# Attention as steps of three parts in a written order on TensorE, in one layer step of a hybrid trunk

## The chip, the cores and the metric

The kernel runs on one core of a Trainium2 chip. The metric is the device time of one execution in microseconds (us): 3321.58 us median of three runs of the kernel before (3320.39 to 3327.34). Engines are named as in the profile: PE is TensorE (matmuls), PEld its weight loads, DVE is VectorE, ACT is ScalarE, POOL is GpSimd, SP issues the DMAs.

## The reference, cut to what matters

Two layers work on 512 latent and 128 prompt tokens of width 1024. Each layer has a feed-forward half step, a mixer and another feed-forward half step; the change is in the mixer. It adds three kinds of heads to the residual stream through one output projection:

```python
x = x + g1 * (0.5 * swiglu(modulate(rms_norm(x, ...), sh1, sc1), ffn1_w1, ffn1_w2))
m, aux = mix_fn(modulate(rms_norm(x, lp['norm_mix']), sh2, sc2))   # [MLA | SWA | GatedDeltaNet] @ w_out
x = x + g2 * m
x = x + g3 * (0.5 * swiglu(modulate(rms_norm(x, ...), sh3, sc3), ffn2_w1, ffn2_w2))

# MLA, 8 heads: every latent token sees all 512 latent tokens and 128 cached ones; prompt sees prompt
s = (einsum(q_nope, k_nope) + einsum(q_rope, k_rope)) * scale
o = einsum(softmax(s), v)
# SWA, 8 heads on 2 key heads: latent tokens see a band of three 128 blocks, the cache and a sink
s = where(valid, einsum(q, k) * scale, -inf);  p = softmax([s_loc, s_ctx, sink])
# gated delta net (GDN), 4 heads, forward and backward: a scan over chunks of 64 tokens
tinv = triangular_solve(eye + lower, eye);  u = tinv @ (v * beta);  wk = tinv @ (kb * exp(gc))
v_new = u_i - w_i @ s;  o_i = qd_i @ s + a_i @ v_new;  s = s * gt_i + kd_i.T @ v_new
```

## The kernel before

All tensors lie with features on the 128 partitions and the 640 tokens (512 latent, 128 prompt) along the free side. The program is written in a framework that places instructions by a simulated schedule: each engine gets one fixed order of instructions, chosen at build time, and waits on semaphores. Tiles come from pools with a number of buffers; a new tile waits until the last reader of the buffer before it is done.

A mixer projects its inputs (`win`, line L104), and does the GDN heads one after the other as groups 0 to 3; a fifth group, group 4, holds the prompt's tokens of all four heads. A group (`gdn_group`, from line 597) has a preparation (norms L615, transposes L634 and L638, decay and products L645 to L672, a 16-step substitution on DVE L692 to L694, its spreading by ACT L710, and products by TensorE L703 with DVE L715 and L720 between them), a recurrence (`step`, L742 to L746) and a tail (L776 to L796). The products of a preparation use two PSUM banks of the kind G; the recurrence uses one bank each of the kinds S0 and S1. PSUM has eight banks: here L=4, G=2, S0=1, S1=1.

After the last projections (`project`, from line 806) the banks of kind L are given up and attention takes their place, with two banks for scores (S) and two for transposes and values (T) in SWA, and, once G, S0 and S1 are given up, with two double banks for scores and four of kind T in MLA.

A head of attention does this: TensorE writes scores of 128 queries into an S tile (L981, L985 mask, L1006 prompt; MLA L1036); DVE takes the row maximum (L905) and its negative (L907 or L909); ACT takes the exponentials (L910) and their sum; DVE takes the reciprocal (L914, with the sink L912, L913); POOL multiplies (L915) into a tile `pr`. Then `pv` transposes `pr` block by block on TensorE into T tiles (L931), ACT copies these to SBUF (L938), TensorE multiplies by the values into another T tile (L942), and ACT copies that to the output (L944). Two blocks of queries share one `pv`; a head has two such pairs, and the prompt's block is a third, smaller one. In the trace a matmul of f32 operands shows as two passes, one of fp32r operands as one.

The order of attention on TensorE is the scheduler's: calls stand in the code as scores, softmax and `pv` of one pair after the other, and the schedule moves them between each other and between the GDN's instructions, as far as tiles allow. Group 4's recurrence and preparation are in the code ahead of attention and are mixed with it.

Outputs of heads go to DRAM (`do`). Before MLA head 2 the buffers of the GDN are given up, a pool for the 24 halves of the outputs is opened in their place, and nine outputs are loaded back (`of<-do`, L507) and split into a high and a low part (ACT L67, DVE L70). MLA heads 2 to 7 are split directly. Then the output projection begins (L104 again, with six L banks).

## Time and profile before

| | |
|---|---|
| median of 3 runs | 3321.58 us |
| the profiled execution's own time | 3325.07 us |
| its span in the trace | 3323.3 us |
| PE busy | 3241.5 us, 98% of the span |
| DVE, ACT, POOL busy | 1886.3, 1384.8, 452.2 us |
| mean granted TensorE clock | 0.987 of 2.4 GHz |
| granted clock and DMA | between 1000 and 1100 us: 0.95 and a DMA share of 0.46 |

A busy PE is not a PE at its peak: ends of matmuls are modelled and overlap, so a stretch that shows hardly any idle time may hold less work than it could. The time is best read stage by stage, by the instructions that begin and end a stage. The stage that is changed begins, in layer 0, near 892 us (group 4's preparation) and ends where the output projection begins, at 1113 us; in layer 1 the same stage runs from 2529 to 2749 us.

### The profile page before, as it was taken

The numbers are of one execution on the slowest core, as the hardware profiler recorded it, in microseconds if no ns is written. First come the engines' busy times: TensorE is split into PE (matmuls) and PEld (weight loads), VectorE is DVE, ScalarE is ACT, GpSimd is POOL, SyncE is SP. The second block draws the span as 40 slices with busy tenths as digits, with TensorE's granted clock in tenths as the row PEclk, the third lists the DMA queues.
The fourth block names the chain that finished last, engine by engine and source line by source line (L and its number), as shares of the span: only waits on it lengthen the run. The fifth ranks groups of instructions, "written<-read, shape, count | busy, mean of one in ns | idle before, by whom it ended". The sixth has DMA issues, their size and how long they took to land.

```text
span 3323.3 us, 56733 instructions
## 1 busy us (share of the span) xinstructions
PE 3241.5 (98%) x22036; PEld 3129.5 (94%) x22036; DVE 1886.3 (57%) x4357; ACT 1384.8 (42%) x3041; POOL 452.2 (14%) x480
## 2 busy tenths in 40 slices
PE   8999999999998999999999999999999989999998
PEld 5999999999887999999999999999998879999998
DVE  4564577686885355643346735477878653433333
ACT  3332334554676433322233323255466763321222
POOL 0000011222343100100000100012114340000000
PEclk9999999999999999999999999999999999999999
DMA  6443453322714224522224534333235242222222
GB/s 212 128 149 116 134 164 127 97 76 91 201 54 138 84 86 133 155 94 72 69 92 143 156 99 139 98 103 110 72 121 152 75 138 74 69 73 74 83 65 76
DMA packets 180190, 364.78 MB, mean 110 GB/s; under 512 B 28112, under 2 KB 68176, under 8 KB 179920
## 3 DMA queue, kind: packets, MB, share of 16 engines
q1 hardware_dynamic: 179920, 361.15, 35.2%
q8 instruction: 173, 2.83, 0.4%
q14 instruction: 97, 0.79, 0.1%
HBM read 315.03 MB, written 46.04 MB: 109 GB/s over the span
## 4 chain that ended last, share of the span: by engine, by line
PE 87%; DVE 6%; ACT 3%; DMA 2%; issue 2%; SPq 0%; POOL 0%; POOLq 0%; DVEq 0%; ACTq 0%
PE psL L104 72%; PE psT L942 3%; PE psG L703 3%; PE psS L1036 2%; PE psT L931 1%; PE psG L275 1%; PE psS L742 1%; DMA of<-do 1%; PE psS L745 1%; ACT pr L910 1%; PE psS L981 1%; DVE hf L169 1%; DMA adaw<-in_wada_dram 0%; DVE wlo L70 0%; PE psS L776 0%
## 5 line engine op out<-in xcount | busy, mean ns | idle before, releaser
L70 DVE TENSOR_TENSOR wlo<-wr,whi 128x512 fp32r<-128x512 f32 (+2 forms) x726 | 494.2, 682 | 709.5 <-ACT whi L67 708.0
L67 ACT ACTIVATE whi<-wr 128x512 fp32r<-128x512 f32 (+2 forms) x726 | 446.2, 616 | 876.2 <-PE psL L104 614.9
L104 PE MATMUL psL<-hb,whi 128*128 128x320 f32 x1968 | 523.8, 313 | 0.7 <-DVE hb L171 0.5
L104 PE MATMUL psL<-hc,whi 128*128 128x320 f32 x1952 | 521.0, 314 | 0.0
L104 PE MATMUL psL<-ha,whi 128*128 128x320 f32 x1856 | 492.3, 312 | 5.0 <-DVE ha L171 3.7
L104 PE MATMUL psL<-hd,whi 128*128 128x320 f32 (+1 forms) x1856 | 486.3, 310 | 1.9 <-DVE hd L171 1.9
L104 PE MATMUL psL<-mh,wlo 128*128 128x320 f32 x1408 | 434.2, 309 | 0.0
L104 PE MATMUL psL<-ml,whi 128*128 128x320 f32 x1408 | 434.0, 309 | 0.0
L104 PE MATMUL psL<-mh,whi 128*128 128x320 f32 x1408 | 432.9, 310 | 0.0
L104 PEld LDWEIGHTS psL<-hb,whi 128*128 128x128 f32 x1968 | 351.9, 189 | 2.6 <-DVE hb L171 1.2
L104 PEld LDWEIGHTS psL<-hc,whi 128*128 128x128 f32 x1952 | 349.4, 189 | 0.8
L104 PEld LDWEIGHTS psL<-ha,whi 128*128 128x128 f32 x1856 | 329.8, 188 | 8.6 <-DVE ha L171 5.7
L104 PEld LDWEIGHTS psL<-hd,whi 128*128 128x128 f32 (+1 forms) x1856 | 328.9, 188 | 5.2 <-DVE hd L171 3.1
L269 DVE SCALAR_TENSOR_TENSOR ada<-adaw,cs,ada 128x512 f32<-128x512 f32 x448 | 313.7, 743 | 0.0
L104 PE MATMUL psL<-hb,wlo 128*128 128x320 f32 (+1 forms) x984 | 307.3, 312 | 0.0
L104 PE MATMUL psL<-hc,wlo 128*128 128x320 f32 (+1 forms) x976 | 305.6, 313 | 0.0
L104 PE MATMUL psL<-hd,wlo 128*128 128x320 f32 (+1 forms) x928 | 287.7, 310 | 0.0
L104 PE MATMUL psL<-ha,wlo 128*128 128x320 f32 (+1 forms) x928 | 287.5, 311 | 0.0
L104 PEld LDWEIGHTS psL<-ml,whi 128*128 128x128 f32 x1408 | 264.0, 188 | 2.8
L104 PEld LDWEIGHTS psL<-mh,whi 128*128 128x128 f32 x1408 | 263.5, 188 | 3.0
L104 PEld LDWEIGHTS psL<-mh,wlo 128*128 128x128 f32 x1408 | 264.1, 188 | 2.0
L273 POOL TENSOR_TENSOR adal<-ada,adah 128x512 fp32r<-128x512 f32 x64 | 89.8, 1404 | 1041.7 <-ACT adah L67 823.3
(299 smaller groups left out, 5612.1 us busy)
## 6 DMA issues: line engine op xcount, KB each, us to landing
adaw<-in_wada_dram SPq DMA_DIRECT2D x288, 256.0 KB, 2.9
wr<-in_w1a_dram SPq DMA_DIRECT2D x88, 512.0 KB, 3.7
wr<-in_w1b_dram SPq DMA_DIRECT2D x88, 512.0 KB, 3.5
wr<-in_win_dram SPq DMA_DIRECT2D x54, 512.0 KB, 3.5
wr<-in_w2a_dram SPq DMA_DIRECT2D x32, 512.0 KB, 4.0
wr<-in_w2b_dram SPq DMA_DIRECT2D x32, 512.0 KB, 3.5
wr<-in_wo_dram SPq DMA_DIRECT2D x16, 512.0 KB, 3.6
dqn<-hd SPq DMA_DIRECT2D x24, 320.0 KB, 3.1
```

Source lines behind the costliest of these rows:

```text
L67: self.nc.scalar.activation(dst, src, AF.Copy)
L70: self.nc.vector.tensor_tensor(dst, src, hi.bitcast(F32), ALU.subtract)
L104: i = nc.tensor.matmul(p[:m, :cw], lhsT=w[:, :m], rhs=r[:, c0:c0 + cw], start=(k == 0 and n == 0), stop=(k == kt - 1 and n == 2))
L169: nc.vector.scalar_tensor_tensor(t[:, c0:c0 + n], self.x[k][:, s], A[:, k, g:g + 1], r[j][:, c0:c0 + n], ALU.mult, ALU.mult)
L269: nc.vector.scalar_tensor_tensor(acc[g], raw, c, acc[g], ALU.mult, ALU.add)
L273: nc.gpsimd.tensor_tensor(lo, acc[g], hi.bitcast(F32), ALU.subtract)
L275: nc.tensor.matmul(ps[:2, :], lhsT=self.sel[:, g, :], rhs=x, start=(g + n == 0), stop=(g + n == 2))
L703: nc.tensor.matmul(p[:, s], lhsT=lhs[:, s], rhs=rhs[:, s], start=True, stop=True)
L742: nc.tensor.matmul(p1[:, :P], lhsT=qw[:, u, c, 64 * d:64 * d + P], rhs=S, start=True, stop=True)
L745: nc.tensor.matmul(p2[:, :P], lhsT=KD_[d][c][:, us], rhs=UU[d][:, us], start=True, stop=True)
L942: nc.tensor.matmul(po[:, oc:oc + w], lhsT=vv[:, vb, :], rhs=hl[ti][:, s0:s0 + w], start=(n == 0), stop=(n == len(place) - 1))
L1036: nc.tensor.matmul(p[:, j, :w], lhsT=x[:96, qc], rhs=y[:96, k0 + j * w:k0 + j * w + w], start=(i == 0), stop=(i == 2))
```

## The change

Attention is now a list of steps. A step is a generator of three parts: the scores and softmax of one pair (or of a prompt block), the transposes with ACT's copies, and the values. `staged` runs through the list and, for step i, issues the scores of step i, then the transposes of step i-3, then the values of step i-4, all in a block in which TensorE's instructions keep the order in which they are written (`manual_schedule(engines={PE})`); the other engines are scheduled as before. GDN's last tail (`norm`, `output`), the widening of the score banks from one to two each (`widen`) and the loading of the nine outputs (`collect`) are steps of the same list. A head's order becomes first pair, prompt, second pair.

The PSUM banks change with it. L and G are both given up ahead of attention, while S0 and S1 stay until `widen`. Attention has four T banks and two S banks from its start: the four T banks are those of L, and the two S banks those of G. In MLA the score tiles take the two S banks and those of S0 and S1. Softmax has more buffers (`sm` 12 for 8; `pr` 6 for the wide tiles and 3 of its own for the prompt's, for 5 in all).

```diff
-        self.enter_banks(G=2, S0=1, S1=1, side="right")
+        scan = self.banks(S0=1, S1=1, side="right")
+        scan.__enter__()
+        self.enter_banks(G=2, side="right")
         self.enter_banks(L=4)
...
         self.leave_banks()
+        self.leave_banks()
         self.hp_close()
...
-        with self.banks(S=2, T=2):
-            self.swa(l)
-            t = tail("S0", "T")
-            next(t)
-        self.leave_banks()
-        self.enter_banks(S=2, T=4)
-        self.mla(l, range(2), hook=lambda: list(t))
+        def widen():
+            last.pop().__exit__(None, None, None)
+            scan.__exit__(None, None, None)
+            last.append(self.banks(S=2))
+            last[0].__enter__()
+            yield
+            yield
...
+        def collect():
+            self.leave()
+            self.wp = self.enter("wo")
+            for i in (8, 9, 10, 11, 4, 5, 6, 7):
+                fetch(i)
+            yield
+            yield
+            fetch(0)
+
+        steps = [*self.swa(l), norm(), widen(), *self.mla(l, 0), output(), *self.mla(l, 1), collect()]
+        for head in range(2, 8):
+            steps += self.mla(l, head, osplit)
+        with self.banks(T=4):
+            last.append(self.banks(S=2))
+            last[0].__enter__()
+            self.staged(steps)
+            last.pop().__exit__(None, None, None)
...
-        sm = lambda n: self.att.tile([P, 2], F32, tag=n, name=self.nm(n), bufs=8)
-        pr = self.att.tile([P, w], F32, tag="pr", name=self.nm("pr"), bufs=5)
+        sm = lambda n: self.att.tile([P, 2], F32, tag=n, name=self.nm(n), bufs=12)
+        pr = self.att.tile([P, w], F32, tag="pr" if w > P else "pp", name=self.nm("pr"), bufs=6 if w > P else 3)
...
             hl.append(f)
+        yield
         po = self.pt("T")
...
+    def staged(self, steps):
+        with self.tc.manual_schedule(engines={PE}):
+            n = len(steps)
+            for i in range(n + 4):
+                for at in (i, i - 3, i - 4):
+                    if 0 <= at < n:
+                        next(steps[at], None)
...
+        def latent(pair):
+            if pair == 0:
+                load()
+            vv, ot = self.pair
+            prs = [fin(n, 0, 2, 320) for n in (2 * pair, 2 * pair + 1)]
+            yield
+            blocks = [(s, [(prs[j], s * P, j) for j in range(2)]) for s in range(5)]
+            yield from self.pv(blocks, vv, ot, r0, pair * 256, 256)
...
+        return [latent(0), prompt(), latent(1)]
```

Two places show what moves. The first is TensorE's order where group 4's preparation begins in layer 0. Before, the first scores of SWA (L981, tiles `psS` from keys `k` and queries `q`) stand between the transposes of group 4's keys (L634) and of its values (L638); `uu` and `kd` belong to group 3's recurrence:

```order
L615 MATMUL psG_9517<-ones,QK_9524 128x2 x4
L634 MATMUL psG_9543<-mats,k_9509 128x128 x4
L745 MATMUL psS_1645_9058<-uu_9035,kd_8841 128x128
L981 MATMUL psS_10521<-k_10508,q_10518 128x256
L981 MATMUL psS_10521<-k_10509,q_10518 128x256
...
L981 MATMUL psS_10538<-k_10508,q_10518 128x384
...
L638 MATMUL psG_9544<-mats,v_9510 128x128 x4
L742 MATMUL psS_1647_9070<-st_9054,wqb_8471 128x128
L645 MATMUL psG_9557<-k_9509 128x128 x4
```

Now, on the same engine, the preparation's instructions follow each other with the recurrence alone between them (L645, L664, L668 and L675 are the old L615, L634, L638 and L645; L772 and L775 the recurrence), and the first scores (L1030) stand behind the preparation's last product (L733, the old L703):

```order
L645 MATMUL psG_9520<-ones,QK_9527 128x2 x4
L664 MATMUL psG_9546<-mats,k_9512 128x128 x4
L775 MATMUL psS_1646_9061<-uu_9038,kd_8844 128x128
L668 MATMUL psG_9547<-mats,v_9513 128x128 x4
L772 MATMUL psS_1648_9073<-st_9057,wqb_8474 128x128
...
L733 MATMUL psG_9794<-vn_9558,TT_9769 128x128 x4
L775 MATMUL psS_1804_9819<-uu_9784,kd_9590 128x128
L772 MATMUL psS_1805_9825<-st_9807,wqb_9511 128x128
L1030 MATMUL psS_10530<-k_10517,q_10527 128x256
```

All of SWA has moved behind the whole of group 4's preparation; 64 rows of TensorE's order that hold no attention stand there now.

The second place is a pair of MLA, again on TensorE. Before, the last scores of a pair (L1036) are followed by values (L942) and transposes (L931) in turn:

```order
L1036 MATMUL psS_12738<-k_12713,q_12716 128x320
L942 MATMUL psT_12625<-pt_12619,vv_12571 128x256 x2
L931 MATMUL psT_12664<-mats,pr_12639 128x128
L931 MATMUL psT_12664<-mats,pr_12655 128x128
...
L942 MATMUL psT_12625<-pt_12621,vv_12571 128x256 x2
L931 MATMUL psT_12669<-mats,pr_12639 128x128
...
L942 MATMUL psT_12625<-pt_12623,vv_12571 128x256
```

Now all scores of a pair stand together, then all transposes (L961) of the pair three steps back, then the values (L973) of the step four back, here a prompt's, and then the scores of the next head (L1102):

```order
L1102 MATMUL psS_12611<-k_12501,q_12504 128x320
L961 MATMUL psT_12627<-mats,pr_12451 128x128
L961 MATMUL psT_12627<-mats,pr_12467 128x128
...
L961 MATMUL psT_12632<-mats,pr_12451 128x128
...
L961 MATMUL psT_12637<-mats,pr_12451 128x128
...
L973 MATMUL psT_12646<-pt_12586,vv_12207 128x128
L1102 MATMUL psS_12661<-k_12652,q_12649 128x320
```

Scores of two pairs, four tiles, have one set of transposes and one short value product between them at this place.

## Rows read from the trace of the kernel before

**Rows 1.** The page, part 1: busy time, share of the span, instructions.

```profile
PE 3241.5 (98%) x22036; PEld 3129.5 (94%) x22036; DVE 1886.3 (57%) x4357; ACT 1384.8 (42%) x3041; POOL 452.2 (14%) x480
```

**Rows 2.** Timeline and chain, stage borders: start us, us, engine line op.

```profile
892.01 1.88 PE L615 MATMUL psG<-ones,QK 128*128 128x2 f32 x16
1113.24 11.87 PE psL L104 x81
2528.87 1.84 PE L615 MATMUL psG<-ones,QK 128*128 128x2 f32 x16
2749.45 30.65 PE psL L104 x209
```

**Rows 3.** Windows: us, busy PE, PEld, DVE, ACT, POOL, PEclk, DMA.

```profile
892.00:969.00 77.00, 70.31 (x494) 62.40 (x493) 63.50 (x245) 51.98 (x164) 34.90 (x39) 0.96 0.36 88
969.00:1004.00 35.00, 34.48 (x239) 30.45 (x239) 23.92 (x87) 28.22 (x87) 13.66 (x16) 1.00 0.21 64
1004.00:1064.00 60.00, 47.88 (x274) 42.23 (x272) 32.27 (x75) 36.09 (x84) 21.03 (x20) 0.91 0.47 134
1064.00:1104.00 40.00, 39.65 (x259) 36.81 (x258) 21.00 (x59) 30.17 (x74) 19.95 (x19) 1.00 0.44 133
2638.00:2700.00 62.00, 51.14 (x290) 44.49 (x289) 32.82 (x78) 38.47 (x90) 22.45 (x21) 0.92 0.49 137
```

**Rows 4.** Groups of instructions, DVE, 892 to 969 us: SWA's four.

```profile
L905 DVE TENSOR_REDUCE mx<-psS 128x1 f32<-128x384 f32 (+2 forms) x27 | 14.9, 553 | 3.7 <-PE psS L985 3.3 <-PE psS L1006 0.2
L913 DVE TENSOR_TENSOR den<-den 128x1 f32<-128x1 f32 x25 | 6.3, 252 | 2.2 <-ACT den L912 1.8
L907 DVE TENSOR_SCALAR nb<-mx,nsink 128x1 f32<-128x1 f32 x27 | 5.5, 204 | 0.3
L914 DVE RECIPROCAL den<-den 128x1 f32<-128x1 f32 x25 | 3.9, 154 | 0.1
```

**Rows 5.** Timeline, preparations of groups 2 (781), 3 (869) and 4 (915).

```profile
781.13 0.31 DVE L683 STREAM_TRANSPOSE u<-w 128x128 f32<-128x128 f32 x1 [0.88 <-ACT w L682]
796.71 0.48 DVE L697 TENSOR_SCALAR X<-X,half 128x128 f32<-128x128 f32 x2
869.61 0.48 DVE L697 TENSOR_SCALAR X<-X,half 128x128 f32<-128x128 f32 x2
890.89 1.06 PE L703 MATMUL psG<-vn,TT 128*128 128x128 f32 x8
915.00 0.29 DVE L683 STREAM_TRANSPOSE u<-w 128x128 f32<-128x128 f32 x1
940.08 0.47 DVE L697 TENSOR_SCALAR X<-X,half 128x128 f32<-128x128 f32 x2
968.72 0.50 PE L703 MATMUL psG<-vn,TT 128*128 128x128 f32 x3
```

**Rows 6.** Timeline and groups, SWA's prompt scores, and recurrence passes between them.

```profile
974.72 0.42 PE L1006 MATMUL psS<-k,q 128*128 128x128 f32 x2
994.32 0.52 PE L1006 MATMUL psS<-k,q 128*128 128x128 f32 x2
L742 PE MATMUL psS<-st,wqb 128*128 128x128 f32 x18 | 3.7, 289 | 0.0
```

**Rows 7.** Chain that ended last, dense MLA: start us, us, passes.

```profile
1078.42 0.87 PE psT L931 x8
1079.29 0.88 PE psS L1036 x6
1080.17 0.87 PE psT L942 x4
```

**Rows 8.** Waits of ACT, 1004 to 1064 us: us in total, times, longest.

```profile
ACT oh L67 <- DMA of<-do: 7.6, 4, 2.5
```

**Rows 9.** Timeline, from the end of one MLA score tile.

```profile
1080.21 0.82 DVE L905 TENSOR_REDUCE mx<-psS 128x1 f32<-128x640 f32 x1 [1.11 <-PE psS L1036]
1081.42 0.88 ACT L910 ACTIVATE pr<-psS,nb,rq 128x640 f32<-128x640 f32 x1
```

More of the change, by code (lines that the diff above doesn't have):

```diff
@@ new lines, in mixer, with norm, output, osplit @@
+        o = {}
+        first, last = tail("S0", "T"), []
+        def norm():
+            next(first)
+            yield
+            yield
+        def output():
+            yield
+            list(first)
+            yield
[6 more added lines that the diff above has]
+            yield
+        def osplit(i, f):
+            hi, lo = (self.wp.tile([P, T], F32R, tag="o", name=self.nm("o"), bufs=24) for _ in range(2))
+            self.split(f, hi, lo)
+            o[i] = (hi, lo)
@@ new lines, in mixer @@
+        for head in range(2, 8):
[5 more added lines that the diff above has]
+            last.pop().__exit__(None, None, None)
+        acm.__exit__(None, None, None)
+        self.hp_open()
+        self.open_x()
+        for k in range(KD):
+            nc.sync.dma_start(self.x[k], self.xd[k])
+        with self.banks(L=6, G=2):
+            order = (8, 9, 10, 11, 4, 5, 6, 7, 0, 1, 2, 3)
+            for n in range(KD):
+                w = self.weight(a['wo'][l, n, :, 8:], 4, P) + self.weight(a['wo'][l, n, :, :8], 8, P)
+                w = w[:4] + w[8:] + w[4:8]
+                self.residual(n, w, [o[i] for i in order], G, True)
@@ L939, in pv @@
             hl.append(f)
+        yield
         po = self.pt("T")
@@ L1011, in mla, with queries @@
-    def mla(self, l, heads, wp=None, osplit=None, hook=None):
-        nc, a, att = self.nc, self.a, self.att
-        for head in heads:
-            r0 = 64 * (head % 2)
-            rows = slice(r0, r0 + 64)
-            q, k = [], []
+            K[kv] = kh, kl, vv
+        def queries(head):
+            r0 = 64 * (head % 2)
+            if head % 2 == 0:
+                Q[head // 2, 'out'] = att.tile([P, T], F32, tag="out", name=self.nm("out"), bufs=2)
+            qh = att.tile([P, T], F32R, tag="q", name=self.nm("q"), bufs=4)
+            for n in range(2):
+                self.move(qh[64 * n:64 * n + 64], self.dsq[head // 2][n][r0:r0 + 64])
+            Q[head] = qh
@@ new lines, in latent @@
+        def latent(head, pair):
+            if pair == 0:
+                if head % 4 == 0:
+                    keys(head // 4)
+                queries(head)
+            kh, kl, vv = K[head // 4]
+            info = []
+            for n in (2 * pair, 2 * pair + 1):
+                p, w, lo, nl = scores(Q[head], kh, kl, n)
+                info.append((fin(head, p, w), lo, nl))
+            yield
+            blocks = [(4, [(info[j][0], info[j][2] * P, j) for j in range(2)])]
+            single = []
+            for b in range(4):
+                parts = [(info[j][0], (b - info[j][1]) * P, j) for j in range(2)
+                         if info[j][1] <= b < info[j][1] + info[j][2]]
+                if len(parts) == 2:
+                    blocks.append((b, parts))
+                elif parts:
+                    single.append((b, parts))
+            ot = Q[head // 2, 'out']
+            yield from self.pv(blocks + single, vv, ot, 64 * (head % 2), pair * 256, 256)
+            if pair == 1 and head % 2 == 1:
+                nc.sync.dma_start(self.do[4 + head // 2], ot)
@@ new lines, in prompt @@
+        def prompt(head):
+            kh, kl, vv = K[head // 4]
+            p = self.pt("S")
+            for n, x in enumerate((kh, kl)):
+                nc.tensor.matmul(p[:, :P], lhsT=Q[head][:, TL:], rhs=x[:, T:], start=(n == 0), stop=(n == 1))
+            pr = fin(head, p, P)
+            yield
+            ot = Q[head // 2, 'out']
+            yield from self.pv([(5, [(pr, 0, 0)])], vv, ot, 64 * (head % 2), TL, P)
+        return [s for head in range(8) for s in (latent(head, 0), prompt(head), latent(head, 1))]
@@ L1017, in mla, with load @@
+    def mla(self, l, head, osplit=None):
+        nc, att = self.nc, self.att
+        r0 = 64 * (head % 2)
+        rows = slice(r0, r0 + 64)
+        q, k = [], []
+        def load():
             for n in range(2):
```

140 lines of the change are left out of this document (48 added, 92 removed).

## The prediction

> **What bounds the kernel now.** I read the page's busy shares first [rows 1]: TensorE shows 98%, DVE 57%, ACT 42%, so a change pays where TensorE's order leaves it short of work. Then the chain of waits and the timeline, for the stage's borders: from the first norm of group 4's preparation to the output projection it is 1113.24 - 892.01 = 221.2 us in layer 0 and 2749.45 - 2528.87 = 220.6 us in layer 1 [rows 2]. Then the windows [rows 3], which show three kinds of stretch. From 892 to 969 us SWA runs beside group 3's recurrence and group 4's preparation: TensorE is busy 70.3 of 77 us, but DVE 63.5, and that is the engine that sets this pace. From 969 to 1004 and from 1064 to 1104 us TensorE is busy 34.5 of 35 and 39.7 of 40 us: nothing is left to win there. From 1004 to 1064 us, where MLA starts and the nine outputs are loaded back, it idles 12.1 of 60 us, at a granted clock of 0.91; in layer 1 (2638 to 2700) 10.9 of 62 us, at 0.92.
>
> So the new order can win only in the first and third kind of stretch. In the third it does what it is good for, distance between scores, transposes and values. In the first it takes SWA out: the S banks are now those of G, so the first score stands behind the last product of group 4's preparation, and TensorE gets group 3's recurrence and that preparation alone. One overlap is given up, another gained.
>
> **The change part by part, for one layer.**
>
> *The preparation alone.* Before, 892.01 to 969.2 us, 77 us. DVE spent 14.9 + 6.3 + 5.5 + 3.9 = 30.6 us of it on SWA's softmax [rows 4]. If all of that and nothing else went, 77 - 30.6 = 46.4 us would be left: the lower bound. For the middle I cut it into legs [rows 5]. Norm to DVE's transpose of the triangles (915.00): 23.0 us; with SWA's reductions out of DVE's queue, about 18. The 16-step substitution, 915.00 to 940.08: 25.1 us; group 2's, with no SWA in the queue, took 796.71 - 781.13 = 15.6; group 3's recurrence still stands between its steps, so 17. Substitution to the last product, 940.08 to 969.2: 29.1 us; group 3's took 891.95 - 869.61 = 22.3, with projections' splits in the queues that are gone here, so 19. Sum 54 us. Upper bound, with the legs as they stand: 23.0 + 17 + 22.3, and three more for a slower TensorE: 65.
>
> *Filling the pipeline.* The first transposes come after seven score tiles through two S banks, and a tile comes free 2.1 us after its scores end (1080.21 to 1081.42 + 0.88, of MLA's wider tiles) [rows 9]. Three and a half such rounds are 7 us if TensorE had nothing else; group 4's recurrence and the scores themselves fill some of it, down to 2. I take 4 us.
>
> *SWA.* Dense SWA runs at 994.32 - 974.72 = 19.6 us for two heads, with 18 passes of L742 and as many of L745 among them [rows 6], at 0.11 us a pass (eight in 1.06 us with the last one's tail [rows 5]), 4.0 us: 7.8 us a head without recurrence. Eight heads are 62.4 us; the 64 passes of group 4's recurrence and 16 of its tail are 8.8. Sum 71.2 us. DVE and ACT were busy 23.9 and 28.2 of 35 us in that stretch [rows 3], so neither takes over; they leave little for a late order.
>
> *MLA.* A head is 24 score passes at 0.147, 21 transposes at 0.109, 20 value passes at 0.217 [rows 7] and five short ones at 0.11 us: 3.5 + 2.3 + 4.3 + 0.6 = 10.7 us, eight heads 85.6. Transposes three steps late find `pr` done, since POOL and ACT get two or three steps, over 5 us. What is not covered: first, the loading. ACT waited 7.6 us for `of<-do` between 1004 and 1064 [rows 8], and ACT's queue still holds those nine splits between the exponentials and copies. When it stands, no score tile comes free, and TensorE is held after one step. I keep 6 us. Second, the order at a head's end: scores of two pairs with only ten transposes and one short value product between them, 2.2 us with the second tile's scores. A tile comes free 2.1 us after its scores [rows 9] if ACT has nothing ahead of the exponential; behind another one of 0.88 us TensorE waits that long. I take 0.6 us a head, 5 us for eight. Both: 11, between 3 (the depth hides the loading) and 16 (as before, and the head ends on top). The last step's copy and values take 1.5 us.
>
> *Buffers.* More `pr` and small tiles let POOL and DVE run ahead. The two dense stretches show no wait that they could take away [rows 3]: 0 us, at most 1 gained.
>
> *Sum.* 54 + 4 + 71.2 + 85.6 + 11 + 1.5 = 227.3 us, against 221.2 and 220.6: +6.1 and +6.7, +12.8 us for both layers. The rest of the program is the same work in the same order. The profiled execution took 3325.07 us (1.8 over its span), so it becomes 3337.9; the runs' median lies 3.5 us under that execution, so I predict 3334 us.
>
> *What two rules say.* The windows show two regimes in one stretch, DVE at 63.5 of 77 us beside TensorE, then TensorE alone [rows 3]. The Trainium skill, Perfetto Trace Analysis, section "Optimization Strategy", advises interleaving regimes whose most-contended engine differs. The trace agrees; by that rule the preparation's separation is the costly part, and at the legs' upper bound of 65 us the sum is 238.3 us a layer, +35 us for both.
>
> **The rivals.**
>
> *Faster.* It decides, by over 0.2%, once preparation and MLA's losses together fall from 65 to 55 us. The preparation is DVE's work alone, 46.4 us, the pipeline fills in 2 and the depth hides the loading, 3: 46.4 + 2 + 71.2 + 85.6 + 3 + 1.5 = 209.7 us a layer, -22.4 for both: 3299 us. For it: every group of the trace has its chain stretched by something in DVE's queue. Against: the chain hops between four engines and group 2's shortest substitution is still 15.6 us [rows 5].
>
> *No change.* The loading is half hidden and head ends cost nothing (5 instead of 11): 221.3 us a layer, 3322 us. For it: 12 us of idle are won in MLA and 54 us of preparation hold TensorE work that the old stretch had to do too. Against: ACT's order keeps the waits.
>
> *Much slower, by the clock.* Where TensorE waited 12 of 60 us, its granted clock was 0.91, and 1.00 in both dense stretches [rows 3]: part of the stretch ran at 1.2 GHz instead of 2.4. In the preparation alone TensorE has some 240 passes of 0.11 us, 27 us of work in 54, so it may sit at 1.2 GHz for most of it. The 96 passes of L703 are on its chain; at 0.11 us more each that is 10.6 us, and with the upper legs without their three us (62) the sum is 62 + 10.6 + 4 + 71.2 + 85.6 + 11 + 1.5 = 245.9 us, +50 for both: 3372 us. Against: in the old stretch, with TensorE waiting too, the clock was 0.96. The Trainium skill, TensorE: Matmul & The Clock Gate, section "HAM oscillation — how this bites in real kernels", says that waits between bursts of matmuls drop the array to half rate at each burst; the 0.91 agrees, and by that rule this rival's time holds.
>
> *It doesn't do what it says.* A depth of three would mean nothing if S, with two tiles, lets TensorE run no further ahead than before. That is the 5 us above; with two pieces of 0.88 us ahead of every such exponential it is 14 us, the sum 236.3 us a layer and the time 3352 us, which lies inside my forecast's range.
>
> **How the numbers follow.** Forecast, with its close variants (+7 to +38 us): 0.41. Faster: 0.31. No change within 6.6 us (0.2%, about what a measurement of this kernel can tell): 0.17. Much slower: 0.11. So slower 0.41 + 0.11 = 0.52, same 0.17, faster 0.31. The forecast's own range is 3329 to 3360. The range for 8 in 10 reaches to the faster rival's 3299 and a little below, to 3297, and up to 3368, most of the way to the clock's rival.
>
> **What would show it.** In the changed profile: no score in the 54 us after group 4's first norm, and the first one near 946 us (right), or near 938 (faster) or past 957 (slower); TensorE's clock in that stretch well under 0.96; the output projection of layer 0 beginning near 1119 us; ACT still waiting for `of<-do` by some 6 us, and TensorE for ACT's exponentials at head ends by 0.6 us a time; a head of MLA at 10.7 us from the third on. I am wrong if the preparation takes under 48 us, or if MLA's start is as dense as its end.

## The result and the profile after

The changed kernel takes 3373.34 us (median of four runs, 3367.8 to 3376.74), the kernel before 3323.07 us beside it: a ratio of 1.0148, 95% interval 1.013 to 1.0167, some 49 us. The forecast was 3334 us; its range for 8 in 10 ended at 3368. The direction was right, the size was not.

The span is 3369.7 us against 3323.3. TensorE's busy time grew by 20 us with the same 22036 passes, so some of them took longer [rows 1]:

```profile
PE 3261.7 (97%) x22036; PEld 3141.6 (93%) x22036; DVE 1895.1 (56%) x4357; ACT 1382.0 (41%) x3041; POOL 454.6 (13%) x480
```

The borders of the stage, from the timeline of TensorE (start us, us, engine line op), to be laid beside [rows 2]; L645 is the old L615 and L105 the old L104:

```profile
892.69 0.98 PE L645 MATMUL psG<-ones,QK 128*128 128x2 f32 x8
1136.88 0.49 PE L105 MATMUL psL<-o,whi 128*128 128x320 f32 x1
2553.93 1.84 PE L645 MATMUL psG<-ones,QK 128*128 128x2 f32 x16
...
2795.92 0.50 PE L105 MATMUL psL<-o,whi 128*128 128x320 f32 x1
```

The stage takes 1136.9 - 892.7 = 244.2 us in layer 0 and 242.0 in layer 1. Before, it took 221.0 and 220.3 by the same two passes of the timeline (the output projection's first at 1112.99 and 2749.21; the chain in [rows 2] begins 0.25 us later): +23 and +22. Outside it no stretch moved by more than 1.2 us; layer 1's stage starts 25 us later, the 23 of layer 0 and 2 of such small differences. So the question is where 244 us go, against the 227.3 of the forecast's sum. The windows, cut where the first score, the first score of MLA, and the loading begin and end (columns as in [rows 3], the last number is GB/s):

```profile
892.70:947.90 55.20, 42.48 (x249) 36.80 (x247) 40.30 (x143) 18.84 (x54) 14.01 (x14) 0.78 0.29 64
947.90:1025.90 78.00, 70.32 (x482) 60.94 (x482) 53.45 (x196) 59.25 (x195) 34.63 (x42) 1.00 0.23 70
1025.90:1047.00 21.10, 17.78 (x118) 16.48 (x118) 11.13 (x31) 12.66 (x32) 8.93 (x9) 1.00 0.33 95
1047.00:1089.00 42.00, 35.25 (x203) 31.55 (x202) 24.18 (x54) 28.11 (x67) 16.66 (x15) 0.92 0.57 168
1089.00:1136.90 47.90, 43.32 (x267) 38.93 (x265) 17.36 (x50) 31.50 (x80) 18.72 (x17) 1.00 0.35 109
```

The reader is to see three things. The preparation is 55 us, as forecast. SWA takes 78.0 us to MLA's first score, where fill and SWA were to take 75.2. MLA takes 21.1 + 42.0 + 47.9 = 111.0 us, where 85.6 + 11 + 1.5 = 98.1 were forecast; in all three of its windows TensorE idles, also in the last one, far from the loading. Before, such late MLA was dense, 39.7 of 40 us [rows 3].

What TensorE waits for, in SWA (947 to 1026 us) and in MLA (1026 to 1137): us in total, times, longest. The last two rows are the kernel before, over its whole stage.

```profile
PE psS L1030 <- ACT pr L940: 5.8, 7, 1.2
...
PE psS L1102 <- ACT pr L940: 12.7, 9, 2.1
...
PE psT L942 <- ACT pt L938: 6.8, 9, 2.9
PE psS L1036 <- ACT pr L910: 3.9, 2, 2.1
```

Before, TensorE waited mostly for copies. Now one kind of wait makes nearly all of it: scores (L1030, L1102) that wait for ACT's exponential (L940), which frees their tile. A dense head of MLA shows how it comes about (L935 takes the maximum, L939 scales it, L968 copies transposed blocks, L973 are the values; timeline of TensorE, DVE and ACT, from the second pair's scores to those of the next head; wait and releaser in brackets):

```profile
1085.88 2.11 PE L1102 MATMUL psS<-k,q 96*128 96x320 f32 x12
...
1087.14 1.71 DVE L935 TENSOR_REDUCE mx<-psS 128x1 f32<-128x640 f32 x2 [1.78 <-PE psS L1102]
1087.83 1.25 PE L961 MATMUL psT<-mats,pr 128*128 128x128 f32 x10
1088.46 1.09 ACT L968 ACTIVATE pt<-psT 128x512 f32<-128x512 f32 x2 [1.82 <-PE psT L961]
1088.76 0.33 DVE L939 TENSOR_SCALAR nb<-mx,rq 128x1 f32<-128x1 f32 x2
1088.92 0.39 PE L973 MATMUL psT<-pt,vv 128*128 128x128 f32 x2
1089.43 0.89 ACT L940 ACTIVATE pr<-psS,nb,rq 128x640 f32<-128x640 f32 x1
...
1090.47 1.14 PE L1102 MATMUL psS<-k,q 96*128 96x320 f32 x6 [1.16 <-ACT pr L940]
```

TensorE has 1.25 + 0.39 us of work between the two heads' scores. In that time DVE reduces both tiles before it scales either (nb at 1088.76, though the first maximum is there near 1088), and ACT copies two transposed blocks, 1.09 us, before the first exponential. The tile is free 3.2 us after DVE began on it, and TensorE stands 1.16 us. Of the two, the copies end last here: the first scaled maximum is there near 1088.9, ACT is at its copies until 1089.4, and its exponential's row shows no wait for DVE. No run moved the copies or the reductions in their queues, so what each of them costs is read from these rows only.

The wait is 1.16, 1.16 and 1.22 us at MLA's last three dense head ends, and 1.03 to 1.25 at the last four of SWA. In the first half of MLA, with the steps without scores and the loading, single waits are 1.4 to 2.1. The distance of two prompts' scores is a head, 12.4 us (timeline of TensorE), where I had 10.7 of passes and 0.6 of wait:

```profile
1095.66 0.64 PE L1102 MATMUL psS<-k,q 96*128 96x128 f32 x3
...
1108.02 0.64 PE L1102 MATMUL psS<-k,q 96*128 96x128 f32 x3
```

### The profile page after: what moved, and what is told of

It is laid out like the page before. It is cut to its first block, busy times and chain, and to the rows that moved or that the text cites. A ratio compares the mean times of both kernels' runs of the same rounds, so it can differ in the third digit from the quotient of the medians.

```text
span 3369.7 us, 56843 instructions
## 1 busy us (share of the span) xinstructions
PE 3261.7 (97%) x22036; PEld 3141.6 (93%) x22036; DVE 1895.1 (56%) x4357; ACT 1382.0 (41%) x3041; POOL 454.6 (13%) x480
## 5 line engine op out<-in xcount | busy, mean ns | idle before, releaser
L105 PE MATMUL psL<-hb,whi 128*128 128x320 f32 x1968 | 523.4, 313 | 0.2
L105 PE MATMUL psL<-hc,whi 128*128 128x320 f32 x1952 | 520.2, 313 | 0.2 <-DVE hc L172 0.2
L105 PE MATMUL psL<-ha,whi 128*128 128x320 f32 x1856 | 491.8, 312 | 5.0 <-DVE ha L172 3.7
L105 PE MATMUL psL<-hd,whi 128*128 128x320 f32 (+1 forms) x1856 | 486.2, 310 | 2.0 <-DVE hd L172 2.0
L105 PE MATMUL psL<-mh,wlo 128*128 128x320 f32 x1408 | 434.2, 309 | 0.0
L105 PE MATMUL psL<-ml,whi 128*128 128x320 f32 x1408 | 434.0, 309 | 0.0
L105 PE MATMUL psL<-mh,whi 128*128 128x320 f32 x1408 | 432.9, 310 | 0.0
L105 PEld LDWEIGHTS psL<-hb,whi 128*128 128x128 f32 x1968 | 351.7, 189 | 1.8 <-DVE hb L172 0.4
L105 PEld LDWEIGHTS psL<-hc,whi 128*128 128x128 f32 x1952 | 348.6, 189 | 1.4 <-DVE hc L172 0.5
L105 PEld LDWEIGHTS psL<-ha,whi 128*128 128x128 f32 x1856 | 329.6, 188 | 8.8 <-DVE ha L172 5.9
L105 PEld LDWEIGHTS psL<-hd,whi 128*128 128x128 f32 (+1 forms) x1856 | 328.6, 188 | 5.6 <-DVE hd L172 3.5
L105 PE MATMUL psL<-hb,wlo 128*128 128x320 f32 (+1 forms) x984 | 307.1, 312 | 0.0
L105 PE MATMUL psL<-hc,wlo 128*128 128x320 f32 (+1 forms) x976 | 305.1, 313 | 0.0
L105 PE MATMUL psL<-hd,wlo 128*128 128x320 f32 (+1 forms) x928 | 287.8, 310 | 0.0
L105 PE MATMUL psL<-ha,wlo 128*128 128x320 f32 (+1 forms) x928 | 287.1, 311 | 0.0
L105 PEld LDWEIGHTS psL<-ml,whi 128*128 128x128 f32 x1408 | 264.0, 188 | 2.8
L105 PEld LDWEIGHTS psL<-mh,whi 128*128 128x128 f32 x1408 | 263.5, 188 | 3.0
L105 PEld LDWEIGHTS psL<-mh,wlo 128*128 128x128 f32 x1408 | 264.1, 188 | 2.0
```

The source lines that it names most:

```text
L105: i = nc.tensor.matmul(p[:m, :cw], lhsT=w[:, :m], rhs=r[:, c0:c0 + cw], start=(k == 0 and n == 0), stop=(k == kt - 1 and n == 2))
```

## The experiments

Three theories were tried. A: what I mis-sized is the wait for a score tile, of which there are two, at a head's end, where little stands between two sets of scores. B: the whole loss is the lost overlap of SWA with group 4's preparation. C: depth hides the chain, and whatever shortens it or holds the written order up costs. All runs are in one table. The ratio is to the kernel before on the same chip; the stage is worked out from the profiled execution, first norm of group 4 to the first pass of the output projection, layer 0 and 1 (before: 221.0 and 220.3). That execution is the fastest of its kernel's runs in several rows (nosplit, overlap23, hybrid and hybnohole among them) and the slowest in noload, so a few us of stage between two rows can be scatter; the ratio is of all runs.

| kernel | median us | ratio, 95% interval | stage us |
|---|---|---|---|
| changed | 3373.3 | 1.0148 (1.013 to 1.0167) | 244.2, 242.0 |
| lag23 | 3349.7 | 1.0065 (1.005 to 1.008) | 232.2, 232.7 |
| lag35 | 3377.4 | 1.0154 (1.0138 to 1.0169) | 245.9, 242.7 |
| s3 | 3360.5 | 1.0108 (1.0089 to 1.0127) | 239.0, 239.6 |
| overlap | 3355.4 | 1.0085 (1.007 to 1.01) | 234.0, 234.6 |
| unstaged | 3363.8 | 1.0105 (1.009 to 1.012) | 237.6, 239.3 |
| freeorder | 3355.2 | 1.0078 (1.0061 to 1.0095) | 236.7, 235.6 |
| noload | 3344.0 | 1.0057 (1.0042 to 1.0072) | 230.9, 232.1 |
| spread | 3352.2 | 1.0081 (1.0066 to 1.0096) | 235.3, 233.2 |
| nosplit | 3337.4 | 1.0046 (1.0031 to 1.0061) | 225.9, 225.7 |
| overlap23 | 3332.9 | 1.0026 (1.0013 to 1.0039) | 225.2, 219.0 |
| hybrid | 3326.1 | 1.0005 (0.9996 to 1.0015) | 218.8, 219.9 |
| nohole | 3343.3 | 1.005 (1.0033 to 1.0067) | 228.7, 229.0 |
| ov23nohole | 3324.6 | 0.9991 (0.9981 to 1.0) | 222.2, 218.5 |
| hybnohole | 3317.6 | 0.9972 (0.9959 to 0.9985) | 216.1, 214.5 |
| hybpool | 3316.2 | 0.9973 (0.9963 to 0.9984) | 217.1, 214.6 |

**lag23: other parts between the heads.**

```diff
-            for i in range(n + 4):
-                for at in (i, i - 3, i - 4):
+            for i in range(n + 3):
+                for at in (i, i - 2, i - 3):
```

> The changed kernel with transposes two and values three steps behind the scores, instead of three and four; no tile, bank or buffer differs. What it changes is which parts stand between the scores of a second pair and those of the next head: ten transposes and ten value products instead of ten transposes and one short product. Theory A (the loss that I mis-sized is the wait for a score tile at head ends, 1.16 to 1.25 us a head in the changed kernel, up to 2.1 us while outputs are loaded): these waits go, a head of MLA comes at 10.8 us instead of 12.0 and one of SWA at 7.7 instead of 8.9, and the time falls by 20 to 36 us, to 3337 to 3353. Theory B (only the lost overlap of SWA with group 4's preparation costs): the time stays within 5 us of 3373. Theory C (depth is what hides the chain, and less of it costs): new waits of TensorE for transposed tiles, time above 3373.

Measured 1.0065 instead of 1.0148: about 27 of the 49 us come back. The waits, from 940 to 1140 us:

```profile
PE psS L1102 <- ACT pr L940: 9.7, 7, 3.7
PE psS L1030 <- ACT pr L940: 1.2, 4, 0.4
```

SWA's waits at head ends are gone (what is left is 0.2 to 0.5 us in its first heads), and it reaches MLA's first score in 72.8 us instead of 78.0. A head of SWA takes 8.2 to 8.4 us instead of 9.1. MLA keeps 0.67 us at every second head, and its dense heads come at 10.8 and 11.6 us in turn instead of 12.4; the rest of its waits stands in its first half, up to the loading's end. Theory B alone can't explain that; A can.

A small piece of work between two sets of scores is still there, in another place: ten transposes and a short product now stand behind a prompt's scores, one short tile, and the next pair's scores don't wait (timeline of TensorE):

```profile
1089.79 1.28 PE L961 MATMUL psT<-mats,pr 128*128 128x128 f32 x10
1090.90 0.39 PE L973 MATMUL psT<-pt,vv 128*128 128x128 f32 x2
1091.05 2.01 PE L1102 MATMUL psS<-k,q 96*128 96x320 f32 x12
```

**lag35: the same distance by more depth.**

```diff
-            f = self.att.tile([P, 512], F32, tag="pt", name=self.nm("pt"), bufs=6)
+            f = self.att.tile([P, 512], F32, tag="pt", name=self.nm("pt"), bufs=7)
...
-                for at in (i, i - 3, i - 4):
+                for at in (i, i - 3, i - 5):
```

> The changed kernel with the transposes left three steps behind the scores and the values five instead of four (one more tile for transposed blocks, seven for six). Then ten transposes and ten value products stand between the scores of a second pair and those of the next head, as in lag23, but the depth is larger, not smaller. Theory A (what costs is how little stands between the scores at a head's end): most of lag23's 24 us come, 3345 to 3357; the tight place is now between a first pair and the prompt's block (ten transposes and a short product), where one tile, not two, waits. Theory C (lag23 won because the parts follow sooner, by the depth): no gain, 3365 to 3378.

No gain: the time lies in theory C's range, and theory A's was missed. In SWA about half of the gain came (75.6 us to MLA's first score, after 78.0 and lag23's 72.8), but in MLA the waits moved, at the same size, to the place that I had thought harmless, a prompt's scores behind a first pair (timeline of TensorE):

```profile
1095.51 2.12 PE L1102 MATMUL psS<-k,q 96*128 96x320 f32 x12
...
1097.47 1.25 PE L961 MATMUL psT<-mats,pr 128*128 128x128 f32 x10
...
1098.56 0.39 PE L973 MATMUL psT<-pt,vv 128*128 128x128 f32 x2
...
1100.17 0.55 PE L1102 MATMUL psS<-k,q 96*128 96x128 f32 x3 [1.22 <-ACT pr L940]
```

Ten transposes and a short product stand there once more, behind two large tiles, and one short tile waits as long as a large one, since it is the first exponential behind the copies that is late. While outputs are loaded one wait reached 6.0 us. So C's reading, that a shallower pipeline is what won, isn't needed: in all three kernels the small piece stands somewhere, and TensorE waits where it follows a pair, two large tiles (changed, lag35), and not where it follows a prompt's short one (lag23).

**s3: a third score tile for SWA, the order untouched.**

```diff
-            last.append(self.banks(S=2))
+            last.append(self.banks(T=4, S=2))
...
-        with self.banks(T=4):
-            last.append(self.banks(S=2))
...
+        last.append(self.banks(T=3, S=3))
```

> The changed kernel (three and four steps behind) with three score tiles and three transpose banks in SWA, in place of two and four; MLA as it was, two double score tiles and four T. Theory A (the wait at a head's end in SWA is for one of only two score tiles): the waits of 1.03 to 1.25 us of SWA's scores go, SWA shortens by 4 to 8 us a layer, and MLA keeps its 1.16 us a head; time 3356 to 3366. If the order of SWA's exponentials in ACT's queue is what is late, whatever the number of tiles, or if three T banks make value products wait for copies: 3370 to 3380.

1.0108: within the range of theory A. The waits, from 940 to 1140 us (the lines have moved up by one):

```profile
PE psS L1101 <- ACT pr L939: 12.4, 9, 2.3
PE psS L1029 <- ACT pr L939: 3.0, 6, 0.8
```

SWA's fell from 1.25 to 0.76 us at the longest, not to zero; from the norm to its last score it takes 8 us less in each layer, of which the stage keeps 5.2 and 2.4, since MLA got 3 to 5 us longer. MLA's tiles were left alone, and it kept all of its 12. Two tiles and the coarse order make the wait together: a third tile takes away about half of SWA's, the better order nearly all.

**overlap, unstaged, freeorder: the bank plan and the written order apart.** overlap gives SWA the banks of the kernel before; unstaged runs each step's parts one after the other and leaves the order to the scheduler; freeorder keeps the staged calls and leaves out the block that fixes the order.

```diff
-        with self.banks(T=4):
-            last.append(self.banks(S=2))
...
+        last.append(self.banks(S=2, T=2))
...
-            self.staged(steps)
+            for s in steps:
+                list(s)
...
-        with self.tc.manual_schedule(engines={PE}):
```

> The changed kernel with the banks of the kernel before until SWA is over: two score and two transpose banks in the place of the four L banks, G, S0 and S1 given up together at the widening. SWA can then begin beside group 4's preparation, in the written order. Theory B (the lost overlap costs some 21 us a layer: preparation and SWA took 112 us from group 4's first norm to MLA before, 133 in the changed kernel): the first score comes within 25 us of that norm instead of 55 us, SWA ends by 15 to 21 us sooner, time 3331 to 3345. Theory A (score tiles at head ends cost it all): the stretch shortens by less than 5 us, time 3363 to 3373. Theory C (two banks for transposes and values hold a written order up, since every value product waits for ACT's copy of a transposed tile): the overlap is won, but 1 us a step or more is lost again in SWA, time 3350 to 3365, with waits of TensorE for ACT's copies that the changed kernel does not have.

> The changed kernel without the written order: each step's three parts are issued one after the other and the scheduler orders TensorE as in the kernel before; banks, buffers and the order of a head's parts stay changed. So it has the lost overlap alone. Theory B (the lost overlap is the whole loss against the kernel before, and the written order is worth nothing): 3368 to 3378, MLA at 108 to 112 us as before. Theory A (the written order itself costs, by its waits at head ends): 3340 to 3358, since these waits go. If the written order gains in MLA what it was meant to gain, this kernel is slower than the changed one: above 3380.

> The changed kernel with the calls in the same staged order, but outside the block that fixes TensorE's order: the scheduler may move instructions between the steps. Theory A (the fixed order of whole steps makes the waits at head ends): it moves scores, transposes and values between each other, the waits of over 1 us at head ends fall to under half, time 3345 to 3360. Theory B (lost overlap only): within 6 us of 3373. A third reading (what is late is ACT's queue, whose order the scheduler sets in all of these kernels): the waits for exponentials stay at 10 us or more a layer.

unstaged carries the lost overlap (with the new buffers and the new order of a head's parts) and stands at 1.0105, about 35 us: 17 a layer; its time lies between the ranges of A and B. From the first norm to MLA's first score it takes 135.4 and 133.4 us, where the kernel before took 115.3 and 113.7: by this border the overlap is worth some 20 us a layer, and MLA, at 102.2 and 105.9, is a little faster than before. My sum had 14 to 16 for it, 129.2 us to that score. The changed kernel is slower still, by 0.0043 or 14 us, and in the traces this stands in MLA (111.0 and 110.9): the written order, as it stands, costs time in place of winning it. freeorder, with the same calls, wins 23 us of the 49 back, and its exponentials hold scores for 3.4 + 0.9 + 1.3 us instead of 12.7 + 5.8 + 0.5, though its value products now wait 5.7 us for ACT's copies. In overlap the first score is back where it was, 4 us behind the norm:

```profile
896.82 0.85 PE L1026 MATMUL psS<-k,q 128*128 128x256 f32 x4 [1.66 <-DMA q<-dsq]
```

but it wins 10 and 7 us a layer, not 17: it reaches MLA's first score 14 and 10 us sooner after the norm, and MLA gives 4 and 2 back, where the head ends stay (11.2 us of waits). Up to there value products wait 3.0 us in all for ACT's copies, with two T banks (theory C, in small).

**overlap23 and hybrid: do the two losses add?** overlap23 is overlap with lags two and three. hybrid orders SWA by the scheduler and only MLA by the written order:

```diff
-        steps = [*self.swa(l), norm(), widen(), *self.mla(l, 0), output(), *self.mla(l, 1), collect()]
+        steps = [*self.mla(l, 0), output(), *self.mla(l, 1), collect()]
...
+        with self.banks(S=2, T=2):
+            for s in self.swa(l):
+                list(s)
+            next(first)
+        self.leave_banks()
```

> The kernel overlap (SWA in the four L banks, beside group 4's preparation) with transposes two and values three steps behind. If the gains of lag23 (-24 us) and overlap (-18 us) against the changed kernel add, 3331 (3326 to 3336): the head ends and the lost overlap are two separate losses. If lag23's gain in SWA does not come, because with two T banks the value products wait for ACT's copies anyway, and only MLA's is had: 3338 to 3348.

> SWA as in the kernel before (in the four L banks, beside group 4's preparation, ordered by the scheduler, though a head's parts in the order pair, prompt, pair), then MLA alone in the written order, two and three steps behind. Between the first norm of group 4 and MLA's end the kernel before takes 221 us a layer; MLA from its first scores to the output projection takes 105.6 and 106.6 us there and 104.2 and 106.7 in lag23. If the written order is worth nothing in MLA as long as the outputs are loaded in one step: 3320 to 3332, no change against the kernel before. If it is worth the 11 us a layer that I had reckoned: 3300 to 3312. If the hand-over costs (MLA's first transposes come only after two steps of scores, where TensorE has nothing else): 3332 to 3345.

overlap23 came out at 3332.9, 1.0026: 1.0148 less the 0.0083 of lag23 and the 0.0063 of overlap is 1.0002, so they nearly add: the head ends and the lost overlap are two losses. hybrid shows no difference from the kernel before: with the overlap back and the head ends eased, the written order in MLA was worth nothing yet.

**noload, spread, nosplit: what holds MLA's second and third head.** All three are edits of lag23: the nine DMAs left out, with a fill by POOL (0.63 us each) in their place; one load in each of nine steps; the loads kept and eight of nine splits left out. noload and nosplit so leave out work that the result needs.

```diff
-            nc.sync.dma_start(f, self.do[i])
+            nc.gpsimd.memset(f, 0.5)
...
+        for k, i in enumerate((8, 9, 10, 11, 4, 5, 6, 7, 0)):
+            steps[n + 1 + k] = along(steps[n + 1 + k], i)
...
-            osplit(i, f)
+            if not o:
+                osplit(i, f)
+            o[i] = o[8]
```

> The kernel lag23 (transposes two, values three steps behind) with the loading of the nine outputs left out: POOL fills each tile with a constant in the place of the DMA, so the output is not the reference's; the nine splits by ACT and DVE stay. In lag23 the stretch of MLA in which the outputs are loaded (1037 to 1069 us in layer 0) holds waits of TensorE of 1.2, 1.9, 3.7 and 0.9 us, in layer 1 1.2, 1.9, 3.6 and 2.5, and the granted clock is 0.96 there. If the loading is what holds ACT and so the score tiles, these waits fall to the 0.7 us of the later heads, and the time falls by 8 to 16 us a layer at most, 3320 to 3340 in all. If it is the nine splits in ACT's queue (0.74 us each) and not the waits for the DMA, the time falls by less than 5 us, 3344 to 3350.

> The kernel lag23 with the nine loads and their splits not in one step (collect) but one in each of nine steps, from the prompt of MLA head 2 on. Loading theory (the waits come from nine loads through two buffers standing together in ACT's queue): the waits of 1.9 and 3.7 us go, 3326 to 3342. If only the number of splits matters, or the two buffers shared with the heads' outputs: the waits move to the later heads and the time stays at 3344 to 3352; if the splits stand between an exponential and the scores that wait for it, above 3352.

> The kernel lag23 with the nine loads kept, but only the first loaded output of the nine split into halves; the output projection uses these halves for all nine, so the output is not the reference's. It takes eight exponential-sized instructions (0.74 us) out of ACT's queue and as many of 0.82 us out of DVE's. noload, without the DMAs but with the splits, stood 3 us under lag23's ratio at most. Split theory: the waits of 1.9 and 3.7 us in MLA's second and third head fall to about 0.7 to 1.2, the clock of that stretch stays at 1.00, and the time falls by 4 to 8 us a layer, 3334 to 3342. If the holes in the list alone make these waits: 3344 to 3352.

Leaving out the loads took 0.0008 of the ratio, less than the intervals tell apart; spreading them took nothing, the waits moved to later heads. Leaving out the splits took 0.0019, some 6 us in all, with intervals that overlap; the profiled executions show twice that, and alike in both layers: MLA takes 99.0 and 98.8 us instead of 104.2 and 106.7. The window of the loading, lag23 first, then nosplit:

```profile
1043.00:1085.00 42.00, 35.47 (x216) 32.40 (x215) 23.29 (x57) 31.97 (x75) 17.71 (x16) 0.96 0.59 174
```

```profile
1043.00:1085.00 42.00, 37.71 (x244) 34.48 (x243) 19.55 (x58) 29.21 (x73) 20.04 (x20) 1.00 0.58 173
```

28 passes more fit into the same 42 us, with the DMAs as busy as before and the granted clock at 1.00 instead of 0.96. But nosplit takes away two things: the splits, by ACT (0.74 us each) and DVE (0.82), in the queues that free score tiles, and with them ACT's waits for the loads, since nothing reads eight of the nine tiles any more. In lag23 ACT waits 3.3 us for a load just ahead of the exponential for which TensorE waits 3.7. noload, in which ACT waits for no load either, kept the splits and took hardly less time than lag23, so most of the gain should be the splits'. That is argued from the traces; by the ratios noload and nosplit can't be told apart (1.0057 and 1.0046). The waits of 1.9 and 1.4 us stay in nosplit, and I can't say by these runs how they divide between the holes in the list and the order of DVE and ACT.

**nohole, ov23nohole, hybnohole, hybpool: no steps without scores.** `norm`, `widen`, `output` and `collect` are done ahead of the scores of an attention step, in lag23, overlap23 and hybrid; hybpool is hybnohole with the nine high halves written by POOL.

```diff
-        steps = [*self.swa(l), norm(), widen(), *self.mla(l, 0), output(), *self.mla(l, 1), collect()]
+        def along(step, *first):
+            for f in first:
+                f()
+            yield from step
+
+        steps = [*self.swa(l), *self.mla(l, 0), *self.mla(l, 1)]
...
+        for k, f in ((-24, (lambda: next(first), widen)), (-19, (lambda: list(first),)), (-18, (collect,)), (-15, (lambda: fetch(0),))):
+            steps[k] = along(steps[k], *f)
```

> The kernel lag23 with norm, widen, output and collect no longer steps of their own but done ahead of the scores of an attention step. In lag23 they are steps without matmuls of attention, so where they pass through the list a part is missing between the scores: in MLA's order the scores of four tiles follow each other with ten transposes only, or with one transpose, and TensorE waits 1.9 and 3.7 us for an exponential there (1050.8 and 1060.1 us; 1.9 and 1.4 or 2.7 us with the loads left out, so it is not the loads). Theory A' (the holes are the same loss as the head ends): these two waits fall to 0.7 us each, 4 us a layer, 3338 to 3345. If the splits in ACT's queue are what holds the exponentials: the waits stay at 1.5 to 4 us and the time at 3346 to 3352.

> overlap23 with the same edit: overlap given back, lags two and three, no steps without scores. If the three losses add (overlap23 stands at 3333, and the holes cost 4 us a layer): 3322 to 3328, no different from the kernel before. If the splits hold the exponentials: 3330 to 3336.

> The kernel hybrid (SWA ordered by the scheduler in the four L banks, then MLA in the written order, two and three steps behind) with the same edit for output and collect. It stands at 3326, no different from the kernel before. If the holes cost 4 us a layer: 3316 to 3321, and it is faster than both kernels. If not: 3324 to 3328.

> The kernel hybnohole (SWA by the scheduler beside the preparation, MLA in the written order two and three steps behind, no steps without scores; 3317.6 us, 0.28% under the kernel before) with the high halves of the nine loaded outputs written by POOL, not by ACT. If ACT's queue is what holds the exponentials there: its wait of 3.3 us (1047.4 us) falls to about 1.2, 3306 to 3314. If POOL is late instead (its multiplication is two steps ahead of the transposes that read it): new waits of TensorE for POOL's tiles, 3318 to 3326.

The first three gained 0.0015 to 0.0035 over their parents, as expected (nohole's 0.0015 is within the intervals, the other two are clear of them), but not for the reason given: where lag23 waits 1.2, 1.9, 3.7 and 0.9 us, nohole waits 1.8, 0.9, 1.4, 0.7 and 2.3, hardly less, while MLA's first score comes about 3 us sooner after the norm. So, as far as the traces show, the holes cost their own length, where the list changes from SWA to MLA, rather than the waits. hybnohole is faster than both kernels, by 0.28% (0.15 to 0.41) than the kernel before; its stage in layer 0 (timeline of TensorE):

```profile
891.93 1.76 PE L630 MATMUL psG<-ones,QK 128*128 128x2 f32 x15
...
1108.06 0.50 PE L105 MATMUL psL<-o,whi 128*128 128x320 f32 x1
```

It still has one wait of 3.3 us among the splits. hybpool takes that wait away, but TensorE then waits 2.7 us for a `pr` that POOL multiplies late: no difference, and a time between the two ranges expected.

## Why the prediction was wrong

*The preparation held.* Its three legs, [rows 5] for before (timeline; L713, L727, L733 are the old L683, L697, L703):

```profile
910.41 0.31 DVE L713 STREAM_TRANSPOSE u<-w 128x128 f32<-128x128 f32 x1
927.54 0.48 DVE L727 TENSOR_SCALAR X<-X,half 128x128 f32<-128x128 f32 x2
946.05 1.06 PE L733 MATMUL psG<-vn,TT 128*128 128x128 f32 x8
947.89 0.68 PE L1030 MATMUL psS<-k,q 128*128 128x256 f32 x4 [0.29 <-DVE uu L760]
```

17.7, 17.1 and 19.6 us against 18, 17 and 19; the first score at 947.9 against 946. In layer 1 it is 53 us. The price of the lost overlap, 14 to 16 us a layer in my sum, is borne out in the main: 20 us to MLA's first score in unstaged, 18 and 17 in the changed kernel. The rule of the Trainium skill, Perfetto Trace Analysis, section "Optimization Strategy", named the costlier part rightly. That unstaged's 35 us equal what I had worked out by it is chance: I had the legs at 65 us there, and they took 55.

*The step that failed is MLA's losses, "I take 0.6 us a head, 5 us for eight", with SWA's "neither takes over" beside it.* I had the place, the two tiles and the releaser right, and priced one exponential ahead. The trace has two copies of ACT and a second reduction of DVE ahead, and the wait is 1.16 to 1.22 us in a dense head of MLA. It costs more than it lasts: such a head takes 12.4 us, where a head of lag23 without a wait takes 10.8, so the passes at 10.7 were right and a head end loses 1.7 us, at that price 13 for eight, where I had 5. In SWA such waits make 5.8 us, where I took none, because a dense SWA before showed no idle time [rows 3]. The scheduler's order there puts transposes and values in turn between the scores. The two rows that I priced it by [rows 9] came from that order too. The exponential follows its reduction by 0.4 us there, and I took this for an empty queue, but three copies stood ahead of it on ACT and were done about when the maximum was scaled (timeline of the kernel before):

```profile
1080.25 1.28 ACT L938 ACTIVATE pt<-psT 128x512 f32<-128x512 f32 x3
```

The rival "it doesn't do what it says" had this mechanism, at 14 us for MLA's head ends; that is close to the 13 that eight dense heads would lose, and SWA's 5.8 come on top of it. lag23 and s3 show it from two sides.

*The loading was named in part.* I kept 6 us for ACT's waits for `of<-do`. ACT does wait for them, 4.9 us in six times (7.6 before [rows 8]), from 1026 to 1137 us:

```profile
ACT o L68 <- DMA of<-do: 4.9, 6, 1.6
```

But leaving the DMAs out of lag23 gave 2 us a layer or less; leaving the splits out, and ACT's waits with them, gave 6 to 7 in the traces, 3 by the ratios. How the loading's loss divides in the changed kernel itself no run shows, since all three were edits of lag23.

*The sum.* Layer 0 is 244.2 against 227.3: 1.2 more in the preparation, 2.8 in fill and SWA, 12.9 in MLA. Some 3 us of MLA's belong to SWA: TensorE does SWA's last 17 passes and four of the GDN's tail behind MLA's first score, and my sum had them ahead of it. So SWA is some 6 us over, about its waits, and MLA some 10. Of MLA's 111.0 us TensorE idles 14.7, against 11 in my sum; the other part of the 10 are passes that took longer than in a dense stretch, behind the waits and in the loading, where ten value passes take up to 3.94 us instead of 2.32 (1067.27 us, granted clock 0.92). By the runs, 9 to 12 us of the stage go with the better lags, and in the traces 6 to 7 more with the splits, which brings it to 226; that this meets the 227.3 is luck, since the terms don't agree one by one.

*The rivals.* Faster fell with the preparation (55.2 us, not 46.4) and with MLA's losses, no change with MLA's losses. "Much slower, by the clock" gave 3372 us, almost the time measured, by luck: the clock did fall in the preparation, but the legs took 55 us and not the 72.6 of that rival.

*What would show it.* Right: the first score, the clock under 0.96 (0.78), ACT's wait for `of<-do` (4.9 for 6). Wrong: the output projection at 1136.9 and not 1119, head ends at 1.2 and not 0.6, a head of MLA at 12.4 us and not 10.7.

## What to carry to other kernels

Where an order is fixed by hand over two score tiles, look for the smallest piece of work between a tile's last write and its next one, go through the queues of every engine that frees it, in their order, and price that; here a deeper pipeline only moved the place. Steps of unequal size should lag by numbers that put a long part behind each large set of scores and leave the short part to a small one, and a step without scores does not belong in the list. Before two stages share banks, add up what their overlap is worth: here it was 17 us a layer in the whole stage, more than the written order won in any of the runs.

## What the runs showed of the hardware

TensorE's clock, alone in the preparation: it was granted 1.00 from 892.7 to 905 us, 0.72 to 918, 0.62 to 931 and 0.80 to 948, while TensorE was busy for 10.2 of 12.3, 8.1 of 13, 8.5 of 13 and 15.8 of 17 us. The first products of L733 behind that stretch ran at the lower of its two levels, 1.2 of 2.4 GHz, nearly to their end, and the 64 passes that follow them without a wait ran at the higher one (row of the timeline, and windows with columns as in [rows 3]):

```profile
931.92 6.78 PE L733 MATMUL psG<-bd,U 128*128 128x128 f32 x32 [3.21 <-ACT bd L740]
...
931.90:935.20 3.30, 3.28 (x15) 3.28 (x16) 1.17 (x2) 1.85 (x5) 0.00 (x0) 0.50 0.00 0
935.20:938.50 3.30, 3.30 (x19) 3.30 (x18) 1.81 (x6) 0.00 (x0) 0.01 (x1) 0.56 0.02 5
938.50:942.80 4.30, 4.30 (x39) 4.19 (x39) 3.83 (x7) 0.00 (x0) 1.01 (x1) 1.00 0.00 0
```

32 passes in 6.78 us, 0.21 a pass, where later ones take 0.13 (eight in 1.06 us, with the last one's tail); so some 2.6 us lost, in a leg that still fitted its term. The Trainium skill, TensorE: Matmul & The Clock Gate, section "HAM oscillation — how this bites in real kernels", has a burst begin at the lower rate behind a wait. The trace agrees: the burst stands behind a wait of 3.21 us and begins at 0.50. In MLA's loading stretch it was 0.92 in the changed kernel, 0.96 in lag23 and 1.00 in nosplit: in the last of these the waits fell by 3 us against lag23 and MLA by 5 in layer 0, so a part of what the splits cost may be the clock that goes down with the waits.
